# The first down projection of a decoder trunk: row fetches, a product's sums, joining copies and the last rows' rounding moved

## The chip, the cores and the metric

The kernel runs on one core of one Trainium2 chip. The metric is the device time of one execution in microseconds (us), the median of several. A measurement of this kernel is told with all its runs, since they differ by up to 0.4%.

A core has a matrix engine (TensorE, PE in the profile, with its weight loads apart as PEld) and four others that run in parallel: VectorE (DVE), ScalarE (ACT), GpSimd (POOL) and SyncE (SP, which here only issues DMAs). Each engine takes its instructions in the order of the program and waits by semaphores for results of the others. Matrix results land in PSUM banks; everything else is in SBUF, filled from HBM by DMAs.

## The reference

One layer of a decoder trunk over 512 rows of 1024 columns: a SwiGLU block, a mixer of sparse attention and a recurrence, a second SwiGLU block, each behind a norm and added to `x`, and a final norm.

```python
def rmsnorm(x, g):
    x32 = x.astype(jnp.float32)
    y = x32 * lax.rsqrt(jnp.mean(x32 * x32, axis=-1, keepdims=True) + EPS)
    return (y * g.astype(jnp.float32)).astype(x.dtype)

def swiglu(x, w_gate, w_up, w_down):
    return (jax.nn.silu(x @ w_gate) * (x @ w_up)) @ w_down
...
x = x + 0.5 * swiglu(rmsnorm(x, ffn1_norm[l]), ffn1_wg[l], ffn1_wu[l], ffn1_wd[l])
x = x + hybrid_mixer(rmsnorm(x, mix_norm[l]), w_in[l], ...)
x = x + 0.5 * swiglu(rmsnorm(x, ffn2_norm[l]), ffn2_wg[l], ffn2_wu[l], ffn2_wd[l])
return rmsnorm(x, final_norm)
```

`hybrid_mixer` begins with one input projection of the normalised rows, `z = h @ w_in`, whose columns are queries, keys, values, an indexer's queries and keys, and gates. Everything is float32. The change concerns the last product of the first line (`@ ffn1_wd`, 2816 to 1024 columns) and the first columns of the mixer's projection.

## The kernel before

**Operands in two parts.** Each float32 operand is cut into a high part of a shorter type (fp32r) and the rest: weights `w` into `wh` (ScalarE, a copy that rounds) and `wl = w - wh` (VectorE); the activations into `ch` and `cl`, or `yh` and `yl` behind a norm, or `cx` where they were made early. A product takes three matmuls: `wh·ch`, `wh·cl`, `wl·ch`. Raw weights arrive as `wr` (512 KB, from `w1d`, by SyncE); the rounded ones live in a ring of three buffers `wh` and three `wl` (1024 columns), so that a new `wh` waits until TensorE is done with the one three before it.

**Seven products.** The first down projection (`block_down`, L1066) multiplies 2x2 blocks in seven products instead of eight, whose operands are sums of blocks. A product has ten single steps, most of them also a joined one, `x`, for what is left over. A step is six matmuls of 128x512 (three for each half `m` of 256 rows); two steps that share a `wh` buffer, a pair, are twelve. The order of products in `steps` is: the joined steps of 1 and 2, then 1, 2, 5 (with its joined one and that of 6), 6, 3 (with those of 3 and 7), 7, the joined one of 4, and 4. Product 2 sums into banks called `aux`, the others into `mm`. The weights of products 5, 6, 3 (`sm`, `sj` for the joined ones) and 7 (`s`) are themselves sums of blocks: an SP load of one block, and on it, as an accumulating DMA issued by GpSimd (a load that adds to what is there), another. The operand `ha` of product 5 is made by such a DMA too, from `cr`, which ScalarE writes. Other operands of the activations are VectorE differences (`ha<-hb,ha`).

**Turned.** This projection is computed with rows on partitions: its banks hold 128 rows by 512 columns. Four fetches (`load_rows`, `xr<-xrow`, 512 KB) bring the rows of `x` in that form; `result1` (VectorE, `xr<-mm,xr`) adds a product's banks to them. Once a quarter of the rows is complete, three helpers follow, for each of two row groups: `spread_row` (a ScalarE copy `xp<-xr` and a transposing DMA `xq<-xp` issued by SyncE), `square_row` (ScalarE, `sq<-xr`, which leaves sums of squares in `ssr` for the norm) and `merge_row` (ScalarE copies `x<-xq`, which join the transposed halves in the layout that the mixer needs). `norm_tile` and `upper_half` then make `yh` and `yl` from `x`. The last quarter of rows is done when product 4 ends: TensorE itself turns them (`turn_rows`, `aux<-ident,xr`), and ScalarE and VectorE make `yh` and `yl` out of the banks.

**The mixer's start.** Its first product is `q` (really the indexer's queries, `mm<-yh,wh` and so on over eight blocks `k`), the second the indexer's keys `wk`, whose 40 columns are widened by two casts. `mixer_fetch`, `mixer_begin` (ScalarE, rounding) and `mixer_prepare` (VectorE, the rest) bring in its weights. The norm's roots come from `norm_steps`: a sum, a Sqrt on ScalarE (which needs its table loaded first), a reciprocal on VectorE and TensorE transposes that spread it over the columns.

**What sets the order.** In the first down projection a table written by hand: `task(i, ...)` in `block_down` and `late1` (L1552 to L1565) name for each step `i` what is written behind its matmuls; the driver loop (L1570 to L1595) runs through the steps, and the last three of product 4 for `m=0` and then `m=1`. So an instruction's place on its engine is set by that table, and its time by what it waits for. In the mixer a planner picks the next item by estimated costs; its order reacts to what comes before. Nearly all instructions go through one helper, so the profile gives L250 for them and L238 for DMA issues; tiles tell them apart.

Of the kernel before, what the change touches and what calls it, by code (L numbers as in the profile page):

```python
# [9 lines left out]
F32 = mybir.dt.float32  # L10
# [4 lines left out]
P = 128  # L15
# [240 lines left out]
def hybrid_kernel(ctx, tc, xt, xrow, vec, w1s, w1u, w1d, wm, wki, wrg, watt, wrnn, wout, w2u, w2d, gf, out):  # L256
# [53 lines left out]
    def psaux():  # L310
        return psum("aux")
# [68 lines left out]
    def waits(which, *tiles, aux=0, att=0, slots=0, key=None, mm=0, tmps=0, late=LATE, rounded=0):  # L380
        return which, tiles, aux, att, slots, key, mm, tmps, late, rounded

    def norm_steps(*sums, blocks=range(NQ), total=None):
        n = len(blocks)
        sd = small.tile([P, NQ], F32, tag="st", name=nm("sd"))[:, :n]
        if total is not None:
            yield waits("DVE", total)
            V.tensor_add(sd, total[:, :n], total[:, n:])
            yield waits("ACT", sd)
            A.activation(sd, sd, AF.Sqrt, scale=1.0 / D, bias=epst)  # L390
        else:
            pc = psaux()
            for i, a in enumerate(sums):
                if i:
                    yield waits("PE", a)
                for j, b in enumerate(blocks):

                    T.matmul(pc[:, j * QB:(j + 1) * QB], a[:, b * QB:(b + 1) * QB], mean, start=i + j == 0,
                             stop=i == len(sums) - 1 and j == n - 1)
            yield waits("ACT", pc)  # L400
            A.activation(sd, pc.rearrange("p (b c) -> p b c", c=QB)[:, :n, 0], AF.Sqrt, bias=epst)
        yield waits("DVE", sd)
        rs = small.tile([P, NQ], F32, tag="m8", name=nm("rs"))[:, :n]
        V.reciprocal(rs, sd)
        yield waits("PE", rs, late=0.1)
        pb = psaux()[:, :n * QB]
        for j in range(n):
            T.transpose(pb[:, j * QB:(j + 1) * QB], rs[:, j:j + 1].to_broadcast([P, P]), ident)
        yield waits("ACT", pb)
        A.activation(rstd[:, blocks[0] * QB:(blocks[-1] + 1) * QB], pb, AF.Copy)  # L410
# [655 lines left out]
    def block_down(wd, plain, pairs, sums, made=None):  # L1066
# [20 lines left out]
        def blocks(b, n):  # L1087
            return wd[b * (pairs // 2) + n]

        units, turned, ra, raws, s3 = {}, {}, {}, {}, {}  # L1090

        def fetch(key, i):
            def load():
# [101 lines left out]
        for i in range(0, len(steps), 2):  # L1195
            st = steps[i]
            p, j = st
            if j == pairs:
                if not made:
                    srcs = [lambda k=k: parts_[k] for k in {1: (0, 1), 5: ("w5", 0), 3: (1, 2), 4: (3,)}[p]]  # L1200
                    task(i - 4, unit(i, *srcs, n=S))
                    continue
                if p in (5, 7):
                    task(i - 4, unit(i, lambda n=(5, 7).index(p): joined[n]))
                    continue
                key, src = ("joined", p), {1: wd[2 * pairs], 4: wd[2 * pairs + 1][:, S:]}[p]
                used.append([i - 4, key, src])
                task(i - 4, unit(i, lambda key=key, c=src.shape[-1]: raws[key][:, :c], n=src.shape[-1]))
                continue
            n = j // 2  # L1210
            assert steps[i + 1] == (p, j + 1) and j % 2 == 0
            if p in (1, 4, 2):
                key = (p, n)
                used.append([i - 4, key, {1: 0, 2: 1, 4: 3}[p] * (pairs // 2) + n])
                srcs = [lambda key=key: raws[key]]
            elif made:
                key = (p, n)
                used.append([i - 4, key, made[p][n]])
                srcs = [lambda key=key: raws[key]]
            elif p == 7:  # L1220
                srcs = [lambda n=n, k=k: s3[n][k] for k in range(2)]
            else:
                srcs = [lambda n=n: sums[n]]
            if p == 1:
                task(j, lambda n=n: difference(n))
            if p == 2:
                task(i, lambda n=n: reduced(n))
            if p == 5 and not made:
                def base(n=n):
                    sums.append(couple(F32, "sm"))  # L1230
                    Q.dma_start(sums[n], blocks(2, n))

                def add(n=n):
                    G.dma_start(sums[n], blocks(3, n), accum_op=ALU.add)

                at = SUMS_AT[n]
                task(at, [("SP", 0.6, base, False)])
                task(at + 3, [("POOL", 1.2, add, False)])
            if p == 7 and not made:
                def base(n=n, k=0):  # L1240
                    s3.setdefault(n, []).append(slot(F32, "s3"))
                    Q.dma_start(s3[n][k], blocks(2, n)[:, k * S:(k + 1) * S])

                def add(n=n, k=0):
                    G.dma_start(s3[n][k], blocks(0, n)[:, k * S:(k + 1) * S], accum_op=ALU.add)

                for k in range(2):
                    task(i + k - 14, lambda base=base, k=k: base(k=k))
                    task(i + k - 12, lambda add=add, k=k: add(k=k))
            if p == 6 and not made:  # L1250
                def second(n=n):
                    G.dma_start(sums[n], blocks(0, n), accum_op=ALU.add)

                task(index[5, j] - 3, second)
            if p == 3 and not made:
                def fourth(n=n):
                    G.dma_start(sums[n], blocks(1, n), accum_op=ALU.add)

                task(index[6, j] - 3, fourth)
            before = {1: 6, 6: 6, 7: i - index[5, j] - 1, 4: i - (index[7, j] if made else index[3, j] + 6)}.get(p, 5)  # L1260
            if p == 6:
                task(i - before - 1, lambda n=n: V.tensor_sub(a(n, lo), b(n, hi), a(n, hi)))
            if p == 4:
                task(i - before - 1, lambda n=n: V.tensor_sub(a(n, lo), b(n, lo), a(n, lo)))
            task(i - before, operand(p, n))
            task(i - 4, unit(i, *srcs))
# [184 lines left out]
    def mixer_begin():  # L1451
        if len(mixer_begun) < len(loads_):
            n, m = KD, columns(loads_[len(mixer_begun)])[1]
            r = mixer_raws[len(mixer_begun)]
            h, l = (wsp.tile([P, WMAX], F32R, tag=t, name=nm(t)) for t in ("wh", "wl"))
            if m == P:
                A.activation(h, r, AF.Copy)
            else:

                v = lambda t, w: t[:, :n * w].rearrange("p (k c) -> p k c", c=w)  # L1460
                rv, hv = v(r, m), v(h, P)
                A.activation(hv[:, :, 0:m], rv, AF.Copy)
                A.activation(hv[:, :, m:64], rv[:, :, 0:64 - m], AF.Copy)
            mixer_begun.append((r, h, l))
# [84 lines left out]
    late1 = {}  # L1549
    then1 = lambda i, f_, *a: late1.setdefault(i, []).append((f_, a))  # L1550

    for i, (s_, half) in zip((1, 2, 8, 14), ((0, 0), (1, 1), (1, 0), (0, 1))):  # L1552
        then1(i, load_rows, s_, half)
    for p, s_, half, at in ((2, 0, 0, (2, 4, 8)), (3, 1, 0, (2, 4, 8)), (7, 1, 1, (1, 3, 7))):
        for m in range(2):
            then1(lasts1[p] + at[0] + m, spread_row, 2 * s_ + m, half)
            then1(lasts1[p] + at[1] + m, square_row, 2 * s_ + m, half)
            then1(lasts1[p] + at[2] + m, merge_row, 2 * s_ + m, half)
    for k in range(KD // 2):
        then1(lasts1[3] + 10 + k, lambda k=k: y.append(norm_tile(k, V_GM, False)))  # L1560
        then1(lasts1[7] + 8 + k // 2, upper_half, k + KD // 2)
    for n in range(RAWS):
        then1(index[4, 3 + 2 * n] - 4, mixer_fetch)
    then1(index[4, 4], mixer_begin)
    then1(index[4, 4], mixer_prepare)  # L1565
    with tc.manual_schedule(engines=ENGINES):
        assert min(d1.tasks) >= 0
        plan.clear()
# [20 lines left out]
        for m in range(2):  # L1589
            for i in range(last, len(steps)):  # L1590
                products1(i, (m,))
            result1(4, m, *ADDS[4][0])
            square_row(m, 1)
        mixer_begin()
        mixer_prepare()  # L1595

    ends = []

    def turn_rows(m):
# [14 lines left out]
        for t in ("pth", "ptl"):  # L1614
            q = ptp.tile([P, NQ * S], F32R, tag=t, name=nm("QI"))
            QI.extend(q[:, j * S:(j + 1) * S] for j in range(4))


    rgw, turning = {}, []
# [280 lines left out]
    def run_jobs():  # L1900
# [3 lines left out]
        for i, job in enumerate(jobs):  # L1904
# [7 lines left out]
            for k in range(n):  # L1912
# [4 lines left out]
                else:  # L1917
# [2 lines left out]
                    T.matmul(ps[:64 + m, :], ws[load][0][:, k * P:k * P + 64 + m], ys[k][0], start=k == 0, stop=k == n - 1)  # L1920
                    if not k:
                        T.matmul(ps[:m, :], ws[load][0][:, k * P:k * P + m], ys[k][1], start=False, stop=False)
                if k == 1 and not at_:
                    mixer_begin()
                if k == 3 and not at_:
                    mixer_prepare()
# [64 lines left out]


    def normalize():
        yield from norm_steps(total=ssr)
        ready.add("norm")
        held = []
        for k in range(KD + 1):
# [566 lines left out]
```

## Time and profile before

| | |
|---|---|
| runs | 1042.16, 1044.78, 1046.05 us, median 1044.78 |
| the profiled execution's own time | 1047.3 us |
| its span in the profile | 1045.5 us |
| mean granted clock of TensorE | 0.996 |
| bytes moved | 209.63 MB, mean 201 GB/s |
| DMA share of SyncE's and ScalarE's queue (q1), of GpSimd's (q0) | 41.8%, 34.4% |
| first down projection from product 2 to the mixer's start | 243 to 356 us of the span |

In rows of single instructions the columns are: start in the span, length, engine, line, operation, output<-inputs, form, how many are drawn together, and in brackets the idle time of the engine before it and what ended it. Matmuls are pipelined: their lengths overlap, so that only the distance of their starts tells the pace.

### The profile page before, as it was taken

Reading aid. Unit: us, or ns where it says so; the run is one execution under the profiler, and the core shown is the slowest. Engines: PE = TensorE matmul, PEld = TensorE weight load, DVE = VectorE, ACT = ScalarE, POOL = GpSimd, SP = SyncE. Lnnn points to the kernel's source line nnn. Section 1 sums busy time; section 2 is a strip of 40 time slices with the busy share of each in tenths; the row PEclk is TensorE's granted clock in tenths of the full one; section 3 lists DMA queues with packets and bytes.
Section 4 is the critical chain, followed back from the end, with each engine's and each line's share of the span. In section 5 each row is a group of like instructions: output and inputs, shape, how many; then the busy total and the mean of one; then the engine's idle time right before and its main releaser. Section 6 shows DMA issues by size and latency. Waiting matters only on the chain.

```text
span 1045.5 us, 15221 instructions
## 1 busy us (share of the span) xinstructions
PE 1029.7 (98%) x5226; PEld 874.8 (84%) x5226; DVE 898.5 (86%) x1529; ACT 721.6 (69%) x1205; POOL 203.9 (20%) x255
## 2 busy tenths in 40 slices
PE   9999999999998999999999999999999999999997
PEld 8898888897776788888888888888998888898886
DVE  7988999986995698999989976777889999889886
ACT  7756766656768658977887775367667666657864
POOL 1613333212240011111011110012422333210000
PEclk9999999999999999999999999999999999999999
DMA  9969999898997363433359987693979998996454
GB/s 353 202 170 215 225 227 223 201 271 237 204 226 180 132 181 101 141 116 106 111 155 274 279 222 209 192 341 56 206 209 226 220 237 199 210 222 226 163 189 162
DMA packets 99677, 209.63 MB, mean 201 GB/s; under 512 B 24976, under 2 KB 32272, under 8 KB 99600
## 3 DMA queue, kind: packets, MB, share of 16 engines
q1 hardware_dynamic: 67376, 145.42, 41.8%
q0 software_dynamic: 31936, 62.93, 34.4%
q8 instruction: 41, 0.67, 0.3%
q10 hardware_dynamic: 288, 0.31, 0.1%
q14 instruction: 36, 0.29, 0.1%
HBM read 187.12 MB, written 25.17 MB: 203 GB/s over the span
## 4 chain that ended last, share of the span: by engine, by line
PE 89%; DMA 5%; DVE 2%; ACT 2%; issue 1%; DVEq 0%; ACTq 0%; POOLq 0%
PE mm L250 67%; PE aux L250 22%; DMA xq<-xp 2%; DMA wr<-w1d 1%; DMA s<-w1d 1%; DVE wl L250 1%; ACT wh L250 1%; DMA ha<-cr 1%; DVE xr L250 1%; PE aux L1332 0%; DVE sj L250 0%; ACT x L250 0%; DVE cl L250 0%; ACT ch L250 0%; DVE o L250 0%
## 5 line engine op out<-in xcount | busy, mean ns | idle before, releaser
L250 DVE TENSOR_TENSOR wl<-wr,wh 128x1024 fp32r<-128x1024 f32 (+3 forms) x154 | 183.3, 1191 | 39.7 <-ACT wh L250 39.1
L250 ACT ACTIVATE wh<-wr 128x1024 fp32r<-128x1024 f32 (+2 forms) x155 | 158.8, 1026 | 44.7 <-PE mm L250 20.3
L250 PE MATMUL mm<-cm,wh 128*128 128x512 f32 (+1 forms) x736 | 167.0, 354 | 0.0
L250 PEld LDWEIGHTS mm<-cm,wh 128*128 128x128 f32 x736 | 126.3, 190 | 15.8
L250 PE MATMUL mm<-yn,wh 128*128 128x512 f32 x420 | 130.8, 393 | 0.0
L250 PE MATMUL aux<-cm,wh 128*128 128x512 f32 (+1 forms) x472 | 119.5, 383 | 0.0
L250 PE MATMUL mm<-cm,wl 128*128 128x256 f32 x608 | 108.3, 282 | 0.0
L250 PEld LDWEIGHTS aux<-cm,wh 128*128 128x128 f32 x472 | 86.0, 188 | 15.6
L250 PEld LDWEIGHTS mm<-cm,wl 128*128 128x128 f32 x608 | 92.2, 190 | 4.7
L250 PE MATMUL mm<-wl,ch 128*128 128x512 f32 (+1 forms) x240 | 93.9, 391 | 1.8 <-DVE wl L250 1.8
L250 PE MATMUL mm<-wh,ch 128*128 128x512 f32 (+1 forms) x240 | 93.3, 389 | 0.5 <-ACT wh L250 0.5
L250 PE MATMUL mm<-wh,cl 128*128 128x512 f32 (+1 forms) x240 | 93.3, 389 | 0.0
L250 PEld LDWEIGHTS mm<-yn,wh 128*128 128x128 f32 x420 | 77.0, 188 | 14.7
L250 PE MATMUL mm<-yn,wl 128*128 128x512 f32 x210 | 81.9, 390 | 0.0
L250 PE MATMUL aux<-cm,wl 128*128 128x256 f32 x456 | 70.5, 282 | 0.0
L250 ACT ACTIVATE wh<-a 128x1024 fp32r<-128x1024 f32 (+1 forms) x68 | 57.1, 842 | 18.2 <-DVE a L250 17.2
L250 DVE TENSOR_TENSOR wl<-a,wh 128x1024 fp32r<-128x1024 f32 (+1 forms) x68 | 64.8, 953 | 5.5 <-ACT wh L250 5.0
L250 PE MATMUL mm<-yh,wh 128*128 128x512 f32 (+1 forms) x168 | 66.9, 402 | 1.4 <-ACT yh L250 1.4
L250 PE MATMUL mm<-yl,wh 128*128 128x512 f32 (+1 forms) x168 | 66.1, 396 | 0.0
L250 PEld LDWEIGHTS aux<-cm,wl 128*128 128x128 f32 x456 | 63.1, 191 | 1.9
L250 PE MATMUL mm<-yh,wl 128*128 128x512 f32 x160 | 62.8, 394 | 0.0
L250 ACT ACTIVATE tu<-mm 128x512 f32<-128x512 f32 (+1 forms) x57 | 28.3, 496 | 43.9 <-PE mm L250 43.8
(379 smaller groups left out, 2346.3 us busy)
## 6 DMA issues: line engine op xcount, KB each, us to landing
wr<-wm SPq DMA_DIRECT2D x39, 512.0 KB, 3.5
w<-w2d SPq DMA_DIRECT2D x20, 512.0 KB, 8.2
wr<-w SPq DMA_DIRECT2D x20, 512.0 KB, 3.5
wr<-w1u SPq DMA_DIRECT2D x19, 512.0 KB, 6.0
s<-w2u SPq DMA_DIRECT2D x36, 256.0 KB, 4.9
wr<-w2u SPq DMA_DIRECT2D x18, 512.0 KB, 6.0
s<-w2u POOLq DMA_DIRECT2D x36, 256.0 KB, 6.5
s<-w1u SPq DMA_DIRECT2D x32, 256.0 KB, 5.0
```

The lines of the kernel that those rows point to most:

```text
L250: return call(*args, **kw)
```

## The change

Four groups of edits, all around the table of the first down projection.

1. **Rows fetched later.** The four `load_rows` move from steps 1, 2, 8 and 14 to step 3, the last step of product 1, the last of product 2 and the first of product 7.
2. **Product 7's sums by VectorE.** Instead of ten loads by SyncE (256 KB each) and ten accumulating DMAs by GpSimd stand twenty loads by SyncE and ten additions of 128x512 by VectorE. A pair's four loads are written 12 and 11 steps ahead of it, its additions 6 and 5 steps ahead.
3. **Joining copies later.** `merge_row` moves from 8 to 11 steps behind the end of product 2, from 8 to 10 behind that of product 3, and from 7 to 8 behind that of product 7; the lower halves' `norm_tile` moves behind them.
4. **Last rows rounded first.** `upper_half` stands between the two halves of product 4's last three steps, with the square of the first last row; the weights of `q` and of `wk` are rounded at steps 4 and 6 of product 4, `wk` in a buffer of its own; a dummy activation there has the Sqrt table loaded ahead; sum, root and reciprocal (`rs1`) stand right behind the last square, and `normalize` only spreads them, as soon as the rows are turned.

```diff
-    def norm_steps(*sums, blocks=range(NQ), total=None):
-        n = len(blocks)
+    def norm_steps(*sums, blocks=range(NQ)):
...
-        if total is not None:
-            yield waits("DVE", total)
-            V.tensor_add(sd, total[:, :n], total[:, n:])
-            yield waits("ACT", sd)
-            A.activation(sd, sd, AF.Sqrt, scale=1.0 / D, bias=epst)
...
         yield waits("PE", rs, late=0.1)
+        yield from spread_root(rs, blocks)
+
+    def spread_root(rs, blocks):
+        n = len(blocks)
         pb = psaux()[:, :n * QB]
...
+                def other(n=n, k=0):
+                    seconds[n, k] = slot(F32, "s1")
+                    Q.dma_start(seconds[n, k], blocks(0, n)[:, k * S:(k + 1) * S])
+
                 def add(n=n, k=0):
-                    G.dma_start(s3[n][k], blocks(0, n)[:, k * S:(k + 1) * S], accum_op=ALU.add)
-
-                for k in range(2):
-                    task(i + k - 14, lambda base=base, k=k: base(k=k))
-                    task(i + k - 12, lambda add=add, k=k: add(k=k))
+                    V.tensor_add(s3[n][k], s3[n][k], seconds.pop((n, k)))
+
+                task(i - 12, base)
+                task(i - 12, other)
+                task(i - 6, add)
+                task(i - 11, lambda base=base: base(k=1))
+                task(i - 11, lambda other=other: other(k=1))
+                task(i - 5, lambda add=add: add(k=1))
...
-    for i, (s_, half) in zip((1, 2, 8, 14), ((0, 0), (1, 1), (1, 0), (0, 1))):
+    for i, (s_, half) in zip((3, lasts1[1], lasts1[2], firsts1[7]), ((0, 0), (1, 1), (1, 0), (0, 1))):
         then1(i, load_rows, s_, half)
-    for p, s_, half, at in ((2, 0, 0, (2, 4, 8)), (3, 1, 0, (2, 4, 8)), (7, 1, 1, (1, 3, 7))):
+    for p, s_, half, at in ((2, 0, 0, (2, 4, 11)), (3, 1, 0, (2, 4, 10)), (7, 1, 1, (1, 3, 8))):
...
-        then1(lasts1[3] + 10 + k, lambda k=k: y.append(norm_tile(k, V_GM, False)))
-        then1(lasts1[7] + 8 + k // 2, upper_half, k + KD // 2)
+        then1(lasts1[7] + 2 + k, lambda k=k: y.append(norm_tile(k, V_GM, False)))
...
-    then1(index[4, 4], mixer_begin)
-    then1(index[4, 4], mixer_prepare)
+    for j in (4, 6):
+        then1(index[4, j], mixer_begin)
+        then1(index[4, j], mixer_prepare)
+    then1(index[4, 6], lambda: A.activation(small.tile([P, 4], F32, tag="st", name=nm("root"))[:, :1], epst, AF.Sqrt))
...
             result1(4, m, *ADDS[4][0])
-            square_row(m, 1)
-        mixer_begin()
-        mixer_prepare()
+            if not m:
+                square_row(0, 1)
+                for k in range(KD // 2, KD):
+                    upper_half(k)
+        square_row(1, 1)
+        sd, rs1 = (small.tile([P, NQ], F32, tag=t, name=nm("rs")) for t in ("st", "m8"))
+        V.tensor_add(sd, ssr[:, :NQ], ssr[:, NQ:])
+        A.activation(sd, sd, AF.Sqrt, scale=1.0 / D, bias=epst)
+        V.reciprocal(rs1, sd)
...
     def normalize():
-        yield from norm_steps(total=ssr)
+        yield waits("PE", rs1, key="rows", late=0.1)
+        yield from spread_root(rs1, range(NQ))
```

On ScalarE, at the start of product 6, where the transposed rows of product 2 (`xq`) are joined: before, the first pair's copies stand between two operands and the rounding of a weight.

```order
L250 ACTIVATE ch_3000<-cr_2699 128x512
L250 COPY x_94<-xq_2919 128x2x256
L250 COPY x_95<-xq_2919 128x2x256
L250 ACTIVATE wh_3012<-sm_2399 128x1024
```

After the change, in the same place:

```order
L250 ACTIVATE ch_2999<-cr_2698 128x512
L250 ACTIVATE wh_3009<-sm_2399 128x1024
L250 ACTIVATE ch_3013<-ha_105 128x512
L250 ACTIVATE ch_3025<-cr_2722 128x512
L250 ACTIVATE wh_3035<-sm_2408 128x1024
L250 ACTIVATE ch_3039<-ha_107 128x512
L250 COPY x_94<-xq_2918 128x2x256
L250 COPY x_95<-xq_2918 128x2x256
L250 COPY x_94<-xq_2932 128x2x256
L250 COPY x_95<-xq_2932 128x2x256
L250 ACTIVATE wh_3063<-sm_2481 128x1024
```

All four copies have moved behind the rounding for the second pair (`wh<-sm_2408`), and stand ahead of that for the third.

On ScalarE, at the change from product 7 to product 4, where the rows of product 3 are joined, before:

```order
L250 ACTIVATE wh_3427<-sj_2689 128x512
L250 COPY x_94<-xq_3359 128x2x256
L250 COPY x_95<-xq_3359 128x2x256
L250 COPY x_94<-xq_3370 128x2x256
L250 COPY x_95<-xq_3370 128x2x256
L250 ACTIVATE wh_3455<-wr_3397 128x1024
```

And after the change:

```order
L250 ACTIVATE wh_3447<-sj_2688 128x512
L250 ACTIVATE wh_3471<-wr_3417 128x1024
L250 COPY x_94<-xq_3376 128x2x256
L250 COPY x_95<-xq_3376 128x2x256
L250 COPY x_94<-xq_3388 128x2x256
L250 COPY x_95<-xq_3388 128x2x256
L250 ACTIVATE wh_3495<-wr_3439 128x1024
```

The rounding of product 4's first weights now precedes the copies.

On VectorE, at the start of product 7, before, with the joined weights of 3 and 7 (`sj`) ahead:

```order
L250 TENSOR_TENSOR wl_3270<-sj_2663,wh_3269 128x512
L250 TENSOR_TENSOR cl_3279<-ha_103,ch_3278 128x512
L250 TENSOR_TENSOR ha_105<-hb_106,ha_105 128x2x256
L250 TENSOR_TENSOR wl_3299<-s_542_3165,wh_3298 128x512
```

After the change, with two tiles `s` for each half:

```order
L250 TENSOR_TENSOR wl_3271<-sj_2659,wh_3270 128x512
L250 TENSOR_TENSOR s_546_3188<-s_546_3188,s_547_3190 128x512
L250 TENSOR_TENSOR cl_3282<-ha_103,ch_3281 128x512
L250 TENSOR_TENSOR s_550_3207<-s_550_3207,s_551_3209 128x512
L250 TENSOR_TENSOR ha_105<-hb_106,ha_105 128x2x256
L250 TENSOR_TENSOR wl_3304<-s_546_3188,wh_3303 128x512
L250 TENSOR_TENSOR wl_3304<-s_550_3207,wh_3303 128x512
L250 TENSOR_TENSOR s_554_3221<-s_554_3221,s_555_3223 128x512
```

Two additions a pair have come between the operands' differences and the weights' rests, in one queue.

More of the change, by code (lines that the diff above doesn't have):

```diff
@@ L381, in waits @@
         return which, tiles, aux, att, slots, key, mm, tmps, late, rounded
-    def norm_steps(*sums, blocks=range(NQ), total=None):
-        n = len(blocks)
-        sd = small.tile([P, NQ], F32, tag="st", name=nm("sd"))[:, :n]
-        if total is not None:
-            yield waits("DVE", total)
-            V.tensor_add(sd, total[:, :n], total[:, n:])
-            yield waits("ACT", sd)
-            A.activation(sd, sd, AF.Sqrt, scale=1.0 / D, bias=epst)
[L391 to L401, printed above, removed]
+    def norm_steps(*sums, blocks=range(NQ)):
+        pc, n = psaux(), len(blocks)
+        for i, a in enumerate(sums):
+            if i:
+                yield waits("PE", a)
+            for j, b in enumerate(blocks):
+                T.matmul(pc[:, j * QB:(j + 1) * QB], a[:, b * QB:(b + 1) * QB], mean, start=i + j == 0,
+                         stop=i == len(sums) - 1 and j == n - 1)
+        yield waits("ACT", pc)
+        sd = small.tile([P, NQ], F32, tag="st", name=nm("sd"))[:, :n]
+        A.activation(sd, pc.rearrange("p (b c) -> p b c", c=QB)[:, :n, 0], AF.Sqrt, bias=epst)
         yield waits("DVE", sd)
@@ L1088, in blocks @@
             return wd[b * (pairs // 2) + n]
-        units, turned, ra, raws, s3 = {}, {}, {}, {}, {}
+        units, turned, ra, raws, s3, seconds = {}, {}, {}, {}, {}, {}
         def fetch(key, i):
@@ L1454, in mixer_begin @@
             r = mixer_raws[len(mixer_begun)]
-            h, l = (wsp.tile([P, WMAX], F32R, tag=t, name=nm(t)) for t in ("wh", "wl"))
+            h, l = (wsp.tile([P, WMAX], F32R, tag=t, name=nm(t)) for t in ("wh", "wl")) if m == P else (couple(F32R, "wk"), None)
             if m == P:
@@ L1616, in turn_rows @@
             QI.extend(q[:, j * S:(j + 1) * S] for j in range(4))
+        ready.add("rows")
     rgw, turning = {}, []
@@ L1922, in run_jobs @@
                         T.matmul(ps[:m, :], ws[load][0][:, k * P:k * P + m], ys[k][1], start=False, stop=False)
-                if k == 1 and not at_:
+                if k == 1 + (not i) and not at_:
                     mixer_begin()
```

## The prediction

> **What bounds the kernel now.** I read the page's busy shares and the chain that ended last, then TensorE's waits, then the span cut into stages.
>
> ```profile
> PE 1029.7 (98%) x5226; PEld 874.8 (84%) x5226; DVE 898.5 (86%) x1529; ACT 721.6 (69%) x1205; POOL 203.9 (20%) x255
> PE 89%; DMA 5%; DVE 2%; ACT 2%; issue 1%; DVEq 0%; ACTq 0%; POOLq 0%
> ```
>
> ```profile
> PE mm L250 <- DVE xr L250: 3.7, 1, 3.7
> PE mm L250 <- ACT yh L250: 1.4, 1, 1.4
> ```
>
> TensorE is busy for 98% of the span and has 89% of the chain. The two longest waits (total, times, longest) are on VectorE's or ScalarE's part of one job: rounding an operand into a high part and a rest, or adding finished banks to the rows. The next view says where (length, busy time of TensorE, weight load, VectorE, ScalarE and GpSimd, granted clock, DMA share, GB/s).
>
> ```profile
> 215.00:243.30 28.30, 28.30 (x163) 24.80 (x161) 22.40 (x33) 14.22 (x24) 1.81 (x3) 1.00 0.94 279
> 243.30:356.00 112.70, 103.63 (x433) 80.89 (x433) 84.77 (x131) 82.56 (x133) 26.15 (x30) 0.97 0.84 189
> 356.00:725.00 369.00, 369.00 (x1696) 305.79 (x1695) 315.47 (x605) 263.87 (x448) 43.72 (x68) 1.00 0.60 178
> ```
>
> From 243 to 356 us stands the first down projection from its second product on, with the start of the mixer; TensorE idles 9.1 us there, and the clock is 0.97. In the 369 us behind, it never idles. What can be won lies in these 113 us. Busy time is not yet lost time, so I take starts of matmuls (start, length of one or more).
>
> ```profile
> 243.11 0.39 PE L250 MATMUL mm<-wl,ch 128*128 128x512 f32 x1
> 254.23 0.39 PE L250 MATMUL aux<-wh,ch 128*128 128x512 f32 x1
> 274.18 0.62 PE L250 MATMUL mm<-wh,cx 128*128 128x512 f32 x2
> 293.75 0.39 PE L250 MATMUL mm<-wh,ch 128*128 128x512 f32 x1
> 307.36 0.61 PE L250 MATMUL mm<-wh,cx 128*128 128x512 f32 x2
> 323.45 0.39 PE L250 MATMUL mm<-wl,ch 128*128 128x512 f32 x1
> 333.18 0.39 PE L250 MATMUL mm<-wh,ch 128*128 128x512 f32 x1
> 347.48 0.40 PE L250 MATMUL mm<-yh,wl 128*128 128x512 f32 x1
> 354.19 0.57 PE L250 MATMUL mm<-yh,wh 128*104 128x512 f32 x1
> ```
>
> From 293.75 to 307.36 five pairs of steps (12 matmuls each) run without a gap: 13.61 us, so 2.72 a pair and 0.227 a matmul. Held against that pace, five places lose:
> - A, 243.11 to 254.23: 11.12 for one matmul and three pairs (8.39): 2.7.
> - B, 254.23 to 274.18: 19.95 for seven pairs (19.04): 0.9.
> - C, 274.18 to 293.75: 19.57 for six pairs (16.32): 3.2.
> - D, 323.45 to 333.18: 9.73 for one matmul, half a pair and one pair (4.31): 5.4.
> - E, 347.48 to 354.19: 6.71 for 13 matmuls (2.95): 3.8, with 0.2 just before, 4.0.
>
> That is 16.2 us. Part of D and E is the clock:
>
> ```profile
> 241.92:245.33 3.41, 2.31 (x9) 1.26 (x8) 1.20 (x2) 1.58 (x2) 0.00 (x0) 1.00 0.94 366
> 327.25:330.67 3.42, 3.12 (x8) 2.48 (x8) 3.21 (x5) 3.23 (x4) 0.00 (x0) 0.50 0.72 201
> 347.73:351.15 3.42, 1.95 (x6) 0.97 (x6) 1.33 (x3) 2.35 (x5) 0.00 (x0) 1.00 0.41 143
> 351.15:354.56 3.41, 3.41 (x9) 2.49 (x8) 1.74 (x4) 1.56 (x3) 0.00 (x0) 0.50 0.03 8
> ```
>
> Twice the clock is 0.50 for one stretch of 3.41 us, once behind D's wait of 3.7 us and once behind a stretch with 6 matmuls where 15 fit; behind one with 9 it stayed at 1.00. Half clock cost about half of the 3.12 us of matmul in D (1.6), and in E six of fifteen matmuls (1.4).
>
> **The change, part by part.** All sums stand against the profiled execution's own 1047.3 us.
>
> *A: the rows fetched later.*
>
> ```profile
> 243.04 1.06 ACT L250 ACTIVATE wh<-wr 128x1024 fp32r<-128x1024 f32 x1 [5.16 <-DMA wr<-w1d]
> 232.23 0.90 SPq L238 DMA_DIRECT2D xr<-xrow  x2
> ```
>
> ScalarE waited 5.16 us for the first raw weights of product 2. SyncE had issued two row fetches (512 KB each) ahead of them. At the 279 GB/s of the stage 215 to 243.3, that 1 MB is 3.8 us of transfer; without it the weights land near 239.1, and rounding is done ahead of the 243.3 at which TensorE wants them. A goes: **−2.7** (bounds −2.7 and 0). One fetch stays early (step 3), and two now stand directly one after the other on SyncE's queue behind product 2's last weights.
>
> *B: what these two meet there.*
>
> ```profile
> 256.23 0.63 ACT L250 ACTIVATE ch<-ha 128x512 fp32r<-128x512 f32 x1 [2.03 <-DMA ha<-cr]
> ```
>
> B is ScalarE waiting 2.03 us for the accumulated operand of product 5. The edit leaves that chain, but puts 1 MB beside it: 5.5 us at the 189 GB/s of the stage 243.3 to 356, of which I let at most half delay the operand (2.7). Best case B vanishes. I take **0** (−0.9 to +2.7), nearer to the row as it is, since TensorE comes there earlier by A, but VectorE and ScalarE by less.
>
> *C: the joining copies of product 2's rows.*
>
> ```profile
> 277.22 0.68 DVE L250 TENSOR_TENSOR ha<-hb,ha 128x512 f32<-128x512 f32 x1
> 277.50 1.26 ACT L250 COPY x<-xq 128x512 uint16<-128x512 uint16 x2 [1.73 <-DMA xq<-xp]
> 279.19 1.04 ACT L250 ACTIVATE wh<-sm 128x1024 fp32r<-128x1024 f32 x1
> 280.27 1.23 DVE L250 TENSOR_TENSOR wl<-sm,wh 128x1024 fp32r<-128x1024 f32 x1 [0.25 <-ACT wh L250]
> ```
>
> The copy waits 1.73 us in order for a transposed row, and behind it stand a rounding and the difference for which TensorE waits. In the changed order both copies stand behind pair 1. Without 1.73 + 1.16 of copy, VectorE's own queue is next: `ha` ends near 277.8, a `cl` of 0.6 (as `ha`) follows, and `wl` starts near 278.4 instead of 280.27. **−1.9**, left 1.3 (bounds −3.2 and 0): the same four copies now meet pair 2.
>
> *The seventh product's sums.* Ten accumulating DMAs of GpSimd become ten plain loads and ten VectorE additions.
>
> ```profile
> 302.18 0.68 DVE L250 TENSOR_TENSOR ha<-hb,ha 128x512 f32<-128x512 f32 x1
> 302.78 1.29 DVE L250 TENSOR_TENSOR wl<-sj,wh 128x512 fp32r<-128x512 f32 x2
> 319.65 0.68 DVE L250 TENSOR_TENSOR wl<-sj,wh 128x512 fp32r<-128x512 f32 x1
> 302.18:320.33 18.15, 18.15 (x82) 15.04 (x81) 15.65 (x26) 12.99 (x24) 6.03 (x9) 1.00 1.14 236
> ```
>
> A tensor-tensor operation of 128x512 follows another after 0.60 us (302.18 to 302.78), so ten are 6.0. A full pair then takes VectorE six operations, 3.6 us, against TensorE's 2.72. Two reserves cover this. VectorE's idle gaps in product 7, from 302.18 to 320.33 (the window's third figure): busy 15.65 of 18.15 us, so 2.5. And its lead: the last pair's first `wl` ended near 319.1 (two wait their turn of 0.60 until the row at 319.65), while TensorE wants it with the pair's third matmul, 323.45 − 11 × 0.227 + 2 × 0.227 = 321.4, so 2.3. 6.0 − 2.5 − 2.3 = **+1.2** (bounds 0 and 6.0 − 2.3 = 3.7). GpSimd's freed time buys nothing: no long wait names it.
>
> *D: the change from product 7 to 4.*
>
> ```profile
> 321.50 2.42 ACT L250 COPY x<-xq 128x512 uint16<-128x512 uint16 x4 [2.05 <-DMA xq<-xp]
> 324.91 1.23 DVE L250 TENSOR_TENSOR wl<-wr,wh 128x1024 fp32r<-128x1024 f32 x1 [4.58 <-ACT wh L250]
> 326.71 1.28 DVE L250 SCALAR_TENSOR_TENSOR xr<-mm,xr 128x512 f32<-128x512 f32 x2
> ```
>
> ScalarE waits 2.05 us for transposed rows, copies for 2.3, rounds product 4's first weights, and only behind their difference does VectorE add product 7's banks, which TensorE awaits to reuse them (the 3.7). Changed, the rounding stands ahead of the copies: its buffer comes free when product 7's fourth pair ends (near 320.9), so `wh` is done by 322, `wl` by 323.2, the banks by 323.8. With VectorE late by product 7's additions, it ends that pair's second `wl` about when TensorE ends the pair, then has `wl` for the joined weights (0.60), for product 4 (1.14) and one bank (0.60) ahead, against the pair's second half (1.36) and what TensorE had waited: 0.2 to 1.0, I take 0.7 left. The 3.7 us gap and the slow clock go: **−4.7** (bounds −5.4, and −3.2 where the clock halves again and 0.6 more stays).
>
> *E: the mixer's start.*
>
> ```profile
> 338.59 1.06 ACT L250 ACTIVATE wh<-wr 128x1024 fp32r<-128x1024 f32 x1 [0.51 <-PE mm L250]
> 345.62 1.66 ACT L250 ACTIVATE wh<-wr 128x320 fp32r<-128x320 f32 x3
> 347.29 1.28 ACT L250 ACT_TABLE_LOAD   x1
> 348.79 0.46 ACT L250 ACTIVATE yh<-aux,vt 128x256 fp32r<-128x256 f32 x1
> ```
>
> Before, casts (1.66) and the Sqrt table (1.28) stood ahead of `yh<-aux`. Now they precede the last rows, and ScalarE's queue behind the last weights reads: `wh` 0.97, copies 2.3, k-weight casts 0.7, table 1.3, its dummy 0.2 (an estimate), a square 0.6 (as `ch` in B), four `yh` 1.65 (0.41 apart, an estimate from the 0.46). From 338.59 that is 346.3; VectorE, in order, then has the last `yl` (0.4) and the last bank (0.6): 347.3. TensorE wants that bank's rows at 344.06 + 0.36 (transposes) + 1.36 (six matmuls) = 345.8: 1.5 late. Then it wants the reciprocal roots, behind the second square, a sum, a `yh` and the root (0.6 + 0.2 + 0.5 + 0.3 + 0.2 = 1.8, the short ones estimated, so 349.1), after 0.36 + 0.68 of work (348.3): 0.8 late. Left 2.3: **−1.7** (bounds −4.0, and −0.3 with 1.4 of half clock). The gaps of 1.5 and 0.8 us leave about as many matmuls in a stretch as the one with 9 that kept the clock, so I take none. The Trainium skill ("TensorE: Matmul & The Clock Gate", section "HAM oscillation — how this bites in real kernels") says: "The abstract rule is "no PE-idle gaps >~3.4µs."" D's 3.71 us agrees; E's second halving, behind a gap of 1.43, goes beyond it. By the rule alone E would stay at −1.7; by the trace it may be −0.3.
>
> *The mixer's order* shifts by some places. TensorE fills 369.00 of 369.00 us there, so no gain; a loss of up to 1.5, of the size of its longest wait at the mixer's start (1.4). I take 0.
>
> Sum: −2.7 + 0 − 1.9 + 1.2 − 4.7 − 1.7 = **−9.8**, 1037.5 in the profiled execution. The median shown (1044.78) is 2.5 below that execution, so 1035.0.
>
> **The rivals.**
> - *All five go*: VectorE's lead suffices and E's queue is short. −16.2: 1028.6. For it: each wait has a named edit. Against: the queues of C and E still hold the same work.
> - *The waits move*: C gains nothing, the sums cost 3.7, D keeps a half clock (−3.2), E −0.3. With A −2.7 that is −2.5: 1042.3. For it: VectorE is busy 15.65 of 18.15 us in product 7 already; against: D's rounding loses its cover of copies altogether.
> - *The fetches don't give way*: the weights stay late for another reason, A stays: 1037.7.
> - *Slower: additions block VectorE.* An addition waits in order for two loads, and every `wl` stands behind it. It is issued six steps (8.2 us) behind its loads.
>
> ```profile
> DMA to landing us min/median/max: 4.9/8.7/16.0
> ```
>
> These landings are product 7's halves now. If loads go out no sooner than their step, each landing beyond 8.2 us holds a pair; five pairs must lose 15.0 us together for slower by over 0.5% (1037.5 to 1052.5), 3.0 each, so it decides from landings of 11.2 us. Halfway to the slowest (16.0), at 12.1, it is 5 × 3.9 = 19.5: 1054.5. Against it: SyncE issued the first of these loads at 275.6, far ahead of use (below).
>
> ```profile
> L238 SPq DMA_DIRECT2D s<-w1d x10: 327/338/467, 275.6 to 299.4; - x10
> ```
>
> **How the numbers follow.** Forecast 0.57 (own range 1031 to 1039.5), all five go 0.13, waits move 0.20, fetches 0.04, slower 0.06. The range, 1029 to 1043, leaves out the slower case, the end of the second rival and half of the first, about 0.2. A measurement of this kernel can tell about 0.5%, 5.2 us: faster is below 1039.6. That holds nearly all of the forecast (0.53), the first rival, the fetches (0.03) and a quarter of the moving waits: 0.74; slower 0.06; the rest 0.20.
>
> **What would show it.** A: no wait of ScalarE on `wr` near 240 and no TensorE gap behind 243. C: a first wait on `wl` shorter, the copies behind `wh` of pair 1. Sums: VectorE without gaps through product 7 and TensorE waits on `wl` of about 1 us in all. D: the wait on `xr` under 1 us, no 0.50 stretch. E: two gaps on transposes, on `xr` and on the roots. I am wrong if waits on `s` loads appear on VectorE, if a 0.50 stretch remains, or if TensorE idles behind 356.

## The result and the profile after

| | before | after |
|---|---|---|
| median of the runs | 1044.1 us (4 runs, 1042.16 to 1046.05) | 1051.28 us (4 runs, 1050.58 to 1052.8) |
| profiled execution, its span | 1047.3, 1045.5 us | 1052.8, 1051.0 us |
| mean granted clock | 0.996 | 0.992 |

The ratio is 1.0071 (95% interval 1.0048 to 1.0093): 0.7% slower, where 1035.0 was forecast. First the same views as before, of the changed kernel: busy shares and the chain from the page, then TensorE's waits.

```profile
PE 1033.4 (98%) x5226; PEld 875.9 (83%) x5226; DVE 904.7 (86%) x1539; ACT 722.5 (69%) x1206; POOL 194.5 (19%) x245
...
PE 91%; DVE 4%; ACT 2%; issue 1%; DMA 1%; DVEq 0%; ACTq 0%
```

```profile
PE mm L250 <- DVE wl L250: 2.4, 6, 0.7
PE aux L250 <- DVE xr L250: 1.9, 1, 1.9
PE aux L250 <- ACT pm L250: 1.5, 1, 1.5
PE mm L250 <- ACT ath L250: 1.2, 1, 1.2
PE mm L250 <- DVE xr L250: 0.8, 1, 0.8
...
PE aux L250 <- ACT pth L250: 0.7, 1, 0.7
PE mm L250 <- DVE atl L250: 0.6, 1, 0.6
```

The 3.7 us on `xr` are gone, and DMAs have nearly left the chain. But `pm`, `pth`, `ath` and `atl` weren't in the list before: these are tiles of the mixer's attention (the weights of the keys, their transposes, and the result that the projections after it need), some 300 us behind the place of the change. The stages of after say how much it is (columns as in the prediction):

```profile
243.30:338.30 95.00, 91.68 (x391) 71.96 (x389) 82.64 (x127) 71.89 (x112) 17.54 (x21) 1.00 0.87 214
338.30:350.00 11.70, 9.27 (x39) 6.95 (x38) 6.42 (x14) 9.14 (x20) 0.00 (x0) 0.85 0.23 78
350.00:560.00 210.00, 210.00 (x953) 173.28 (x952) 182.75 (x351) 167.50 (x278) 24.90 (x45) 1.00 0.49 148
560.00:640.00 80.00, 79.52 (x383) 66.07 (x382) 69.69 (x164) 49.22 (x98) 12.05 (x15) 1.00 0.92 242
640.00:660.00 20.00, 15.69 (x52) 11.21 (x52) 11.41 (x23) 8.45 (x16) 0.81 (x1) 0.74 0.58 151
```

And the same two last stages of before, whose mixer starts some 5 us later:

```profile
565.00:645.00 80.00, 80.00 (x386) 66.48 (x385) 64.91 (x151) 50.47 (x99) 11.50 (x14) 1.00 0.93 247
645.00:665.00 20.00, 20.00 (x90) 16.58 (x89) 16.58 (x25) 9.23 (x13) 2.44 (x3) 1.00 0.74 202
```

Where TensorE started 90 matmuls in 20 us, it now starts 52, with 4.3 us idle and a clock of 0.74. At 0.227 us a matmul the 38 that are missing would be 8.6 us. The rows of TensorE there, in after:

```profile
643.23 0.60 PE L250 MATMUL aux<-ident,pm 128*128 128x128 f32 x4
645.38 0.66 PE L250 MATMUL aux<-ident,pm 128*128 128x128 f32 x4 [1.55 <-ACT pm L250]
646.72 0.49 PE L250 MATMUL aux<-pth,VV 128*128 128x512 f32 x1 [0.69 <-ACT pth L250]
...
651.62 0.80 PE L250 MATMUL mm<-ath,wh 128*128 128x512 f32 x1 [1.20 <-ACT ath L250]
653.05 0.79 PE L250 MATMUL mm<-atl,wh 128*128 128x512 f32 x1 [0.64 <-DVE atl L250]
```

The last attention head goes back and forth between TensorE, ScalarE and VectorE, and nothing is left to do meanwhile: the next product in TensorE's order is the one that needs it. Before, 21 matmuls of the recurrence's projection stood between the last attention product and `mm<-ath,wh`. In after none does.

To see all places at one scale, I sum over TensorE what each distance of successive starts has over the dense pace (0.227 us for 512 columns, 0.111 for a transpose). In us, one profiled execution each:

| kernel | up to 256 (A) | 256 to 275 (B) | 275 to 300 (C) | 300 to 365 (product 7, D, E) | 560 to 700 (attention's end) | median |
|---|---|---|---|---|---|---|
| before | 2.6 | 0.8 | 3.1 | 9.6 | 1.4 | 1044.1 |
| after | 0.0 | 2.3 | 1.2 | 7.6 | 11.4 | 1051.3 |
| e1 | 0.0 | 1.8 | 1.3 | 7.8 | 1.4 | 1042.1 |
| e2 | 1.3 | 0.5 | 2.6 | 5.7 | 9.5 | 1051.7 |
| e3 | 0.0 | 1.8 | 1.2 | 7.7 | 26.8 | 1066.1 |
| e4 | 2.4 | 0.7 | 3.2 | 7.3 | 15.5 | 1057.7 |
| f1 | 0.0 | 0.0 | 1.2 | 8.4 | 1.4 | 1042.2 |
| f2 | 0.0 | 1.7 | 1.3 | 5.6 | 1.4 | 1038.5 |
| f4 | 0.1 | 2.9 | 1.3 | 7.8 | 1.4 | 1043.3 |
| g1 | 0.0 | 0.0 | 1.1 | 4.3 | 1.3 | 1037.4 |
| g2 | 0.0 | 0.0 | 1.5 | 2.1 | 1.3 | 1034.8 |
| g3 | 0.0 | 0.0 | 2.4 | 1.6 | 8.9 | 1045.6 |
| h1 | 0.1 | 2.3 | 1.3 | 7.8 | 4.2 | 1049.2 |

(e1 to h1 are the experiments below, run in three batches, each with runs of before beside it: medians 1044.19 for e1 to e4, 1044.20 for f1 to g1, 1043.00 for g2, g3 and h1. Up to 256 leaves out the program's start. In h1, matmuls whose results nobody reads count as work.) Ahead of the mixer the change does win: 16.1 us of loss become 11.1. At the attention's end it loses 10.0.

### The profile page after: what moved, and what is told of

It reads as the page before. It is cut to its first block, busy times and chain, and to the rows that moved or that the text cites. A ratio compares the mean times of both kernels' runs of the same rounds, so it can differ in the third digit from the quotient of the medians.

```text
span 1051.0 us, 15262 instructions
## 1 busy us (share of the span) xinstructions
PE 1033.4 (98%) x5226; PEld 875.9 (83%) x5226; DVE 904.7 (86%) x1539; ACT 722.5 (69%) x1206; POOL 194.5 (19%) x245
## 4 chain that ended last, share of the span: by engine, by line
PE 91%; DVE 4%; ACT 2%; issue 1%; DMA 1%; DVEq 0%; ACTq 0%
PE mm L250 68%; PE aux L250 23%; DVE cl L250 1%; DVE wl L250 1%; DVE xr L250 1%; DVE ha L250 1%; ACT wh L250 0%; ACT x L250 0%; DMA wr<-wm 0%; PE aux L1336 0%; DMA s<-w1d 0%; DVE s L250 0%; DVE sj L250 0%; DVE yl L250 0%; DVE ptl L250 0%
## 5 line engine op out<-in xcount | busy, mean ns | idle before, releaser
L250 PEld LDWEIGHTS mm<-yn,wh 128*128 128x128 f32 x420 | 77.3, 188 | 15.3
L250 PE MATMUL mm<-yh,wh 128*128 128x512 f32 x160 | 64.0, 402 | 0.0
L250 PE MATMUL mm<-yl,wh 128*128 128x512 f32 x160 | 62.5, 393 | 0.0
```

The lines of the kernel that those rows point to most:

```text
L250: return call(*args, **kw)
```

## The experiments

Theory O: the planner, fed with other times at the mixer's start, orders the mixer anew, so that the last attention has no other work behind it; that costs the time. Rival S: the attention's chain on VectorE and ScalarE is as long as it is, and an earlier start of the mixer is merely lost there. What follows compares orders on TensorE by its rows, tile by tile.

**e1: the change with the mixer's order of before.** The first three groups of edits stay, and of the fourth only this:

```diff
             result1(4, m, *ADDS[4][0])
-            square_row(m, 1)
+            if not m:
+                square_row(0, 1)
+                for k in range(KD // 2, KD):
+                    upper_half(k)
+        square_row(1, 1)
         mixer_begin()
         mixer_prepare()
```

> Changed: rows fetched later, product 7's sums by VectorE, joining copies later, and of the last edit only the upper halves between the two halves of product 4's last steps. Left as before: the weights of wk, the Sqrt table and the roots. TensorE's order in the mixer is then row by row that of before. Theory O (the mixer's new order, in which the last attention stands behind all other products, cost the time): the gain of 4.5 to 6 us ahead of the mixer stays, loss between 560 and 700 us at most 1.5 us, median about 1038.5. Rival S (the attention's own chain on VectorE and ScalarE bounds the mixer, so an earlier start is lost there again): TensorE waits for pm, pth or ath for about as long as it starts earlier, median about 1044.

Measured: 1042.11 us (10 runs), ratio to before 0.9983 (0.9971 to 0.9995). Its stage at the attention's end:

```profile
640.00:660.00 20.00, 20.00 (x90) 16.57 (x89) 16.64 (x25) 9.23 (x13) 1.91 (x3) 1.00 0.71 204
```

Full, although TensorE came there 5 us earlier than in before, and no wait on `pm`, `pth` or `ath` is left in the list: S falls by the trace. The time alone would not decide: 1042.1 lies nearer to S's 1044 than to O's 1038.5. Against after it is 9.2 us by the medians. The rest of O's number was too good: 5.2 us less loss in the profiles, but only 2.1 in the timed runs. The profiled execution of before (1047.3) lies above all 13 runs that were made of before beside e1 (1041.32 to 1045.84).

**e2: the fourth group alone**, on the kernel before.

> Changed: only the fourth group (last rows rounded first, wk and Sqrt table ahead, roots early) on the kernel before; the mixer's order is row by row that of after, but the mixer starts no earlier than before. Theory O: the attention's end loses 9 to 11 us as in after, and with nothing gained ahead the median is about 1054.5. Rival S: nothing was gained ahead, so nothing is lost there; median 1044 to 1046.

Measured: 1051.71 us (1049.64 to 1052.41), ratio 1.0066 (1.0045 to 1.0088). The loss at the attention's end came with the order (9.5), without the first three groups. It is 3 us less than O said. That nothing is gained ahead was wrong: ahead of the mixer its profile has 10.1 us of loss where before had 16.1.

**e3: the changed kernel with another number in the planner** (`SLACKI = 2.0` for 2.5), which puts 60 matmuls of other work behind the last attention product.

> The changed kernel with one number of the planner changed, the slack for the indexer's items from 2.5 to 2.0; on TensorE 60 matmuls of other products then stand between the last attention product and the first product that needs it (21 before, 0 in after). Theory O: the wait at the attention's end and the slow clock behind it go, median about 1041. Rival S: the chain is as long as it was, median about 1051.

Measured: 1066.05 us, ratio 1.021 (1.0189 to 1.0231). Both theories missed. There is almost no loss behind 640 us, but TensorE idles ahead of it, at the attention's steps from 585 to 620 us:

```profile
PE aux L250 <- ACT pm L250: 8.2, 4, 3.2
```

So work behind the last head is no good measure of an order. This order has moved the idle time forward, and made it larger. What counts, it seems, is whether each step of a head has other work beside it; no run tests that by itself.

**e4: the roots alone.** On the kernel before, only `rs1` behind the last square and `normalize` with `spread_root`, as in the diff of the change. The first down projection is that of before, the mixer's order is a third one.

> Changed: only that the roots of the norm are made right behind the last square and spread as soon as the rows are turned; the first down projection is that of before, the mixer's order changes (the last attention behind all other products, as in after). Theory O: 8 to 11 us lost at the attention's end, median 1052 to 1055. Rival S: median 1043 to 1045.

Measured: 1057.69 us, ratio 1.0124 (1.009 to 1.0158). Ahead, its profile lost 13.6 us where before lost 16.1 (the gain is at D and E), and at the attention's end 15.5 (3.5 us in one wait on `pm`): far more than was gained, so S falls again, and O was if anything too mild. One edit of the change stands in the mixer itself and in none of the four groups: its first product calls `mixer_begin` one block `k` later. After, e2, e3 and h1 have it; e4 and g3 (below) lose at the attention's end without it. What the planner's order does to the attention can be seen on VectorE in the selection of the keys, which the last heads need. Its first and last steps of before and of after:

```profile
404.84 0.43 DVE L250 MAX8 m<-ha 128x8 f32<-128x256 f32 x1 [0.19 <-POOL ha L250]
604.24 0.68 DVE L250 MATCH_REPLACE8 hb<-m,hb 128x512 f32<-128x512 f32 x1
```

```profile
426.23 0.41 DVE L250 MAX8 m<-ha 128x8 f32<-128x256 f32 x1
616.73 0.67 DVE L250 MATCH_REPLACE8 hb<-m,hb 128x512 f32<-128x512 f32 x1
```

The mixer of after starts 5 us earlier, and its selection starts 21 us and ends 12 us later. In e1, with the order of before, it ends at 599.18, 5 us earlier than in before. In e4 it starts at 402.37, before that of before, and ends at 612.04. So a late end goes with the loss; why the planner orders it so was not tried.

**h1: the waits filled.** The changed kernel with matmuls whose results are overwritten: `for _ in range(6): nc.tensor.matmul(pt, VV[0][:, :P], VV[0], start=True, stop=True)` ahead of the last transposes, three such ahead of the last attention product, and eight ahead of the first product that needs it.

> The changed kernel with 17 matmuls whose results are overwritten, put where TensorE waits at the attention's end: 6 ahead of the last transposes, 3 ahead of the last attention product, 8 ahead of the first product that needs it (3.9 us in all, inside waits of 4.8 us). Theory C (about half of the 9.4 us lost there is the slow clock that the idle stretch brings on): the half-clock stretches between 645 and 658 us go, the loss falls to about 5 us, the median to about 1047. Rival: the loss is waiting alone, or the clock halves all the same; median 1051 or more.

Measured: 1049.17 us (1047.37 to 1049.76), ratio 1.0057 (1.0038 to 1.0075). After, and then h1, in the same stretches of 3.41 us:

```profile
648.01:651.42 3.41, 2.40 (x6) 1.32 (x4) 0.33 (x2) 0.97 (x2) 0.28 (x1) 0.50 0.78 126
651.42:654.84 3.42, 2.58 (x5) 1.78 (x6) 3.34 (x8) 2.65 (x5) 0.00 (x0) 0.50 0.15 28
654.84:658.25 3.41, 3.41 (x9) 2.63 (x8) 1.20 (x2) 0.00 (x0) 0.00 (x0) 0.51 0.35 119
```

```profile
648.01:651.42 3.41, 3.41 (x16) 2.77 (x16) 0.98 (x4) 1.67 (x4) 0.26 (x1) 1.00 0.78 131
651.42:654.84 3.42, 2.82 (x13) 2.06 (x12) 3.39 (x6) 1.96 (x3) 0.00 (x0) 1.00 0.12 23
654.84:658.25 3.41, 3.41 (x17) 2.83 (x16) 2.68 (x5) 1.20 (x2) 0.00 (x0) 1.00 0.51 187
```

All three slow stretches are gone, so that the slow clock follows from the idle time. Its price is smaller than I had said: 3.0 us by the spans of the two profiles (1051.0 and 1048.0). The timed runs give 2.1 by the medians and 1.0 when each is held against before beside it, and their intervals overlap, so they do not settle it. By the profiles it is three tenths of the 10.0 that the attention's end lost; the larger part is waiting.

**f1, f2, f4: the terms ahead of the mixer**, each one edit on e1, with the mixer's order of before. f1 puts the second and third row fetch at `lasts1[2] + 4` and `firsts1[6]`.

> As e1, but the second and third row fetch no longer directly behind product 2's weights: four steps behind the end of product 2, and at the first step of product 6. Theory B (the 1 MB beside the accumulating DMAs delays the operand of product 5): TensorE's loss between 256 and 275 us falls from 1.8 to 0.9 or less, the accumulations land in a median of about 6.3 us again, median time 1041. Rival: the operand is late for ScalarE's or GpSimd's own queue; the loss stays 1.8 and the time 1042.

Measured: 1042.22 us, ratio 0.999 (0.9975 to 1.0005). The loss of B went altogether (1.8 to 0.0). The accumulating DMAs `ha<-cr` landed, from e1 to f1:

```profile
DMA to landing us min/median/max: 3.8/7.3/8.8
```

```profile
DMA to landing us min/median/max: 3.8/4.0/6.3
```

So the two fetches beside them did delay the operand (in after the median was 8.4, before 6.3). The timed runs don't show the 1.8 us: by the time alone the rival was right.

f2 gives product 7's sums back to GpSimd, as before the change.

> As e1, but product 7's sums by GpSimd's accumulating DMAs as before. Theory V (VectorE is the bound in product 7 by the ten additions): TensorE's loss between 300 and 323 us falls from 2.8 to under 0.5, median about 1039.5. Rival: the loss there comes from loads or from ScalarE, and stays; 1042.

Measured: 1038.54 us (6 runs, 1038.3 to 1040.06), ratio 0.9961 (0.9945 to 0.9976); the loss between 300 and 323 us fell from 2.8 to 0.4. That is 3.6 us under e1 by the medians and 2.3 by the ratios, whose intervals just overlap. The ten additions cost what VectorE has no room for, as argued, and nothing paid for them.

f4 rounds the weights of `wk` and loads the Sqrt table ahead, as the change does, through the engines' own calls, so that the planner books `wk` where it stood.

> As e1, with the weights of wk rounded and the Sqrt table loaded ahead as in the changed kernel, but unseen by the planner, so that the mixer's order stays that of before; the roots as before. Theory O: the attention's end stays without loss, the mixer's start loses 2 to 3.5 instead of 5.0, median about 1040. Rival S: what the earlier start gains is lost at the attention's end, 1042.

Measured: 1043.26 us, ratio 0.9995 (0.9981 to 1.0008). No loss at the attention's end, so that O holds; but nothing was won at the mixer's start either:

```profile
PE aux L250 <- DVE xr L250: 3.6, 2, 2.9
```

Casts and table now delay the `yh`, VectorE waits with their `yl`, and the last rows' addition stands behind these in its queue. The wait on `yh` has become one on `xr`.

**g1, g2, g3: what is left when the parts that cost are taken out.** g1 is before with the fetches of f1, the joining copies of products 2 and 3 later, and `wk` and table ahead as in f4 (the table at step 1 of product 4).

> Only the parts that paid: rows fetched later (and apart), joining copies of products 2 and 3 later, wk rounded and the Sqrt table loaded ahead unseen by the planner; product 7's sums, the end of product 4, the roots and the mixer's order as before. Theory O with the single terms: TensorE's loss ahead of 365 us falls from 16.2 to 4 or less, no loss at the attention's end, median 1034 to 1037. Rival S: 1042 to 1044.

Measured: 1037.42 us, ratio 0.9946 (0.9927 to 0.9966). The loss ahead is 5.4, not 4, and none is added at the attention's end (1.3).

> As g1, with the Sqrt table loaded in product 7, where ScalarE has room, instead of at step 1 of product 4. In g1 TensorE waited 0.7 us for wh and 0.5 us for wl behind that load. Theory: these two waits go, the rest stays; 1036, 1 to 1.5 us under g1. Rival: the waits move to the next weights; 1037.4.

Measured: 1034.84 us (1034.38 to 1037.32), ratio to before, which ran at 1043.0 beside it, 0.993 (0.9912 to 0.9948): faster than both kernels. Against g1 it is 2.6 us by the medians, 1.7 by the ratios, whose intervals overlap. Its start and end of the mixer:

```profile
332.00:344.00 12.00, 10.96 (x54) 8.20 (x54) 7.13 (x15) 8.80 (x20) 0.00 (x0) 1.00 0.38 123
...
630.00:660.00 30.00, 30.00 (x134) 24.84 (x133) 24.33 (x36) 12.04 (x18) 2.44 (x3) 1.00 0.72 200
```

g3 has the Sqrt table in product 7, as g2. So against g2, and not g1 as its expectation says, it moves only the four `upper_half` behind the last rows' additions, which the planner sees.

> As g1, with the four upper halves behind the last rows' additions instead of ahead of them. On VectorE the additions then wait for nothing but TensorE; but the planner sees the upper halves later, and orders the mixer anew: the last attention stands behind all other products, as in the changed kernel. Theory O: 1 us won at the mixer's start, 8 to 11 us lost at the attention's end, median 1043 to 1047. Rival S (the order doesn't matter): 1036.

Measured: 1045.57 us (10 runs, 1042.55 to 1049.88), ratio 1.0025 (1.0007 to 1.0042). Ahead of the mixer it loses about as much as g2 (4.0 us for 3.6), and yet it is 10.7 us slower by the medians of the same batch. At the attention's end its profile loses 8.9 us for g2's 1.3, and the list of waits has again:

```profile
PE aux L250 <- ACT pm L250: 2.2, 1, 2.2
```

The profiled execution was the fastest of the ten (1042.55); what the others lose more was not seen. It is a fourth order, as unlucky as the others, made by moving four operations.

## Why the prediction was wrong, step by step

- **The mixer's order: the step that failed.** The prediction put it at 0, with "a loss of up to 1.5, of the size of its longest wait at the mixer's start". It cost 10.0 us in the profile, 9.2 by the medians of after and e1. That TensorE filled 369.00 of 369.00 us said only that the order of before covers every wait there, and nothing about another order. A wait from elsewhere in the trace bounds nothing here, since the attention's chain had never been seen uncovered. Of the prediction's own signs of being wrong two came: a 0.50 stretch remained, and TensorE idled behind 356 us. In the profiles the sum was to be −9.8 and came out as +5.5; of the 15.3 between, 10.0 are the order, 2.3 are E and 1.5 are B.
- **A** (−2.7): 2.6 to 0.0. Right in size, with a margin that the working did not have: the weights were to land near 239.1, and ScalarE still waited for them until 241.74 (row below), just early enough for the 243.3 at which TensorE wants them.

```profile
241.74 1.06 ACT L250 ACTIVATE wh<-wr 128x1024 fp32r<-128x1024 f32 x1 [2.00 <-DMA wr<-w1d]
```

- **B** (0, bounds −0.9 to +2.7): 0.8 to 2.3, and f1 shows the fetches as the cause. Within its bounds, 1.5 above the value taken.
- **C** (−1.9): 3.1 to 1.2. Right.
- **Product 7's sums** (+1.2): of the 2.7 between 300 and 323 us, 1.6 stand in product 7 and 1.1 at D's wait on `xr` (0.8). Near enough; f2 gives 2.4 by the profile and 2.3 to 3.6 by the timed runs for both together.
- **D** (−4.7, 0.7 left): 5.4 to 1.1. Right, and the half clock there went.
- **E** (−1.7): 4.2 to 4.8. The two gaps came as worked out, 1.93 for 1.5 and 0.36 for 0.8, but the clock halved behind them (0.57 in the row below). The prediction had named this 1.4 us and not taken it. In e2, with the same edits and the clock at 1.00 from 327.2 us on, this place lost 1.4, so the edits themselves can pay. f4 won nothing with the casts and the table ahead. In g1 and g2 the upper halves stand ahead of the casts, and from 300 us on TensorE lost 4.3 and 2.1 us in all; the table in product 7 is what sets g2 apart.

```profile
344.80:348.00 3.20, 3.20 (x11) 2.63 (x10) 1.26 (x3) 2.56 (x5) 0.00 (x0) 0.57 0.00 0
```

- **The base.** Terms were read from one profiled execution at the top of its kernel's runs, with a half-clock stretch at both D and E. e1 won 5.2 us by the profiles and 2.1 by the timed runs; the base is the likely reason.
- **The rivals.** None of the four was it. The slower one (additions blocked by their loads) did not occur: neither TensorE's nor VectorE's list of waits has one on `s` loads.

## What to carry to other kernels

Where a planner fixes an order from its own estimates, a change ahead of it can change that order even if nothing in it is touched (e4 and g3 did, e1, f1 and f2 did not): compare the order behind the change, row by row, and either keep it or count its loss as unknown in size. In a stretch in which the bounding engine is full, ask how much work covers the longest chain of other engines there; a new order can take that cover away. And a gain ahead is not yet a gain: by the timed runs all four new orders tried here (those of after, e3, e4 and g3) gave back more than was gained.

## What the runs showed of the hardware that I had not expected

The slow clock of TensorE followed waits far shorter than the 3.71 us of before's D: in after it was 0.50 in the stretches from 648.01 on (above), behind this one, in which TensorE worked half of the time and no wait was longer than 1.55 us.

```profile
644.60:648.01 3.41, 1.72 (x7) 1.09 (x8) 1.38 (x2) 1.32 (x3) 0.54 (x1) 0.99 0.29 107
```

What fits all the profiles is how much TensorE worked in a stretch, not its longest wait. Cut at the clock's own switches, the stretches of 3.41 us between 20 and 1000 us of all 13 profiles show it: at full clock, each of the 15 in which TensorE was busy for 1.63 us or less was followed by one at 0.50, and none with 1.98 us or more was; of the five between (1.85 to 1.95) one was.

The runs of one kernel vary along with it: of 13 runs of before made beside g2, the three with a mean clock of 0.999 took 1040.59 to 1041.13 us, the three with 0.996 took 1041.73 to 1047.13.
